# Split weights: low parts formed by a negating copy on ScalarE and an adding transfer, in place of a subtraction on VectorE

## The chip, the cores and the metric

The program runs on one core of a Trainium2 chip. The time is the device time of one execution, in microseconds; of several executions the median is given. The engines of the core work at the same time and wait for each other by semaphores: TensorE (PE for its matmuls, PEld for its weight loads), VectorE (DVE), ScalarE (ACT), GpSimd (POOL) and SyncE (SP, which only issues transfers here).

## The reference

Two request groups (512 and 256 tokens, 768 in all) go through two layers with shared weights, all in float32. Layer 0 mixes tokens with windowed attention, layer 1 with a gated convolution of width 3.

```python
for i in range(DEPTH):
    j = i // N_MIXERS
    h = rms_norm(x, norm_mix[i])
    if i % N_MIXERS == 0:
        x = x + window_attention(h, attn_w_qkv[j], attn_w_o[j], attn_sink[j], band_bias, in_window)
    else:
        x = x + short_conv(h, conv_w_in[j], conv_w[j], conv_w_out[j])
    h = rms_norm(x, norm_mlp[i])
    x = x + jnp.square(jax.nn.relu(h @ mlp_w_up[i])) @ mlp_w_down[i]
    gate = jax.nn.sigmoid(rms_norm(x, norm_ple[i]) @ ple_w_gate[i])
    x = x + (p[i] @ ple_w_proj[i]) * gate
return rms_norm(x, final_norm)
```

The model width is 1024, the hidden width of the MLP 4096, and p has 256 columns.

## The kernel before

**Split operands.** The matmuls take float32r operands. To keep float32 precision each operand is split: its high part is the value rounded to float32r, its low part is what the rounding left. A product of weight w and activation x is then three matmuls for each block of 128 rows: high w with high x, high w with low x, low w with high x, in this order (`group2`, line 123, for two halves of 384 tokens; `group`, line 131, for pieces of up to 512 tokens). The low part of a weight is so first read by the third matmul of its first block, that is the fifth matmul where the tokens are two halves.

**Weights.** A weight tile is 128 rows by up to 1024 columns. `fetch` (line 87) loads it from HBM by SP's queue into `wraw`, of which there are three. `weight` (line 92) takes two tiles, `whi` and `wlo`, of which there are two each, and calls `split` (line 81):

```python
first = act.activation(hi, src, AF.Copy)
dve.tensor_tensor(lo, src, hi.bitcast(F32), ALU.subtract)
```

ScalarE so writes the high part with a rounding copy, and VectorE the low part as raw less high. With two buffers a weight can be split while TensorE works with the one before; the split waits until TensorE has read the older tile in that buffer for the last time.

**Who calls `weight`.** With a source in HBM and the tag "w": the queries and keys of attention and the projections there, the output weights `w_o`, the last group's down-projection of each MLP (`last_down`), the gates (`ple`, and two in `last_ple`), the convolution's inputs (`mixer_conv`: products c, u and b for each of eight blocks) and its output (`project_add`). Three calls have no source, since their load was written apart at the program's start, and one has the tag "z". The other products of the MLPs form sums of weight blocks first, with splits of their own (class `Weights7`), in the same `whi` and `wlo` buffers where their tag is none; they do not call `weight`.

**What sets the order.** Each engine runs its instructions in a fixed order. In the first part of attention, in the MLPs with `last_down`, and at the end the order on ScalarE, VectorE and TensorE is that of the code; in attention, the output product, the gates and the convolution a scheduler chooses it when the program is built. In `last_down` four chunks of weights follow each other; the next chunk's split is called at the head of a chunk's turn, and in ScalarE's order it stands behind the norm (`xs_ple`, `sq`) of the two blocks of the chunk before. The norm waits for VectorE's residual add (line 813), which waits for TensorE. GpSimd sets three columns of each z to zero in the convolution (line 1330) and does nothing else behind the program's start.

Of the kernel before, what the change touches and what calls it, by code (L numbers as in the profile page):

```python
# [11 lines left out]
F32 = mybir.dt.float32  # L12
F32R = mybir.dt.float32r
AF = mybir.ActivationFunctionType
ALU = mybir.AluOpType
# [32 lines left out]
def trunk_kernel(ctx: ExitStack, tc: tile.TileContext, a: dict, out: bass.AP):  # L48
    nc = tc.nc
    act, dve, pe = nc.scalar, nc.vector, nc.tensor  # L50
# [30 lines left out]
    def split(hi, lo, src):  # L81

        first = act.activation(hi, src, AF.Copy)  # L83
        dve.tensor_tensor(lo, src, hi.bitcast(F32), ALU.subtract)  # L84
        return first.ins

    def fetch(src):
        raw = wp.tile([P, CH], F32, name="wraw", bufs=3)
        nc.sync.dma_start(raw[:, : src.shape[1]], src)
        return raw  # L90

    def weight(src, n, raw=None, tag="w"):

        m = CH if src is None else src.shape[1]
        if raw is None:
            raw = fetch(src)
        pool, bufs = (wp, 2) if tag == "w" else (more, 1)
        hi, lo = (pool.tile([P, CH], F32R, tag=f"{tag}{p}", name=f"{tag}{p}", bufs=bufs) for p in ("hi", "lo"))
        split(hi[:, :m], lo[:, :m], raw[:, :m])
        return blocks(hi[:, :m], n), blocks(lo[:, :m], n)  # L100


# [63 lines left out]
    def blocks(t, n):  # L166

        m = t.shape[1] // n
        return [t[:, i * m : (i + 1) * m] for i in range(n)]
# [284 lines left out]
    def mixer_attention():  # L454
# [52 lines left out]
        with tc.manual_schedule(engines=order):  # L507
# [24 lines left out]
            for k in range(2):  # L532
# [5 lines left out]
                part0[1].append(pl[:])  # L538
            w0 = blocks(hi[:], 2), blocks(lo[:], 2)
            w1 = weight(None, 2, raw=w1)  # L540
            for i in range(KB):
                step(0, i, (w0, w1)[i // 4], part0, "L", i % 2)
                norm.block(i, xin(i))
                if i == 3:
                    wk = weight(None, KB, raw=wk)
                    wq = [fetch(a["w_q"][0])]
# [4 lines left out]
            dve.tensor_tensor(brow[:], bp[:HEADS, :], mk[:], ALU.add)  # L551
            kps = list(products(terms_of(wk, xs)))
            wq[0] = weight(None, KB, raw=wq[0])
            ss = norm.sum_squares(psum)

# [815 lines left out]
    w = [weight(a["w_o0"][2], 4)] * 2  # L1371
# [108 lines left out]
```

## Time and profile before

| | |
|---|---|
| time, median of 3 runs | 1717.21 us (1716.59 to 1718.06) |
| span of the profiled execution | 1715.4 us |
| HBM read, written | 123.10 MB, 10.48 MB |
| PE granted clock | 0.97 to 1.00 in all stages up to 1628 us |

The stages, from the trace: start and first projection 0 to 60 us, attention 60 to 280, its output product 280 to 312, MLP of layer 0 from 312, with `last_down` from 771 to 805, gates 805 to 873, convolution 873 to 1075, its output 1075 to 1142, MLP of layer 1 1142 to 1628, gates and final norm to the end.

In the rows of the profile, a group of instructions gives line, engine, operation, the tile written and the tiles read, shapes, the count, then busy time and mean duration in ns, then idle time of the engine before them and who ended it. A row of the timeline gives start, duration, engine, line and operation, and in brackets the idle time before it with its releaser.

### The profile page before, as it was taken

How to read it: one execution, taken by the hardware profiler on the slowest of the kernel's cores; microseconds unless marked ns; L12 is line 12 of the kernel's file. 1: busy time of each engine (PE TensorE's matmuls, PEld its weight loads, DVE VectorE, ACT ScalarE, POOL GpSimd, SP SyncE). 2: the span in 40 equal slices, each digit the busy share in tenths (PEclk: the TensorE clock that was granted, in tenths of full speed). 3: DMA queues.
4: the chain of work that ended last, by engine and by line, in shares of the span. 5: the costliest groups of instructions: out<-in, count | busy, mean ns of one | idle time of the engine just before them, and what ended most of it. 6: DMA issues, size and time to landing. Idle time of an engine off the chain costs nothing.

```text
span 1715.4 us, 24192 instructions
## 1 busy us (share of the span) xinstructions
PE 1673.1 (98%) x9542; PEld 1615.8 (94%) x9542; DVE 1348.2 (79%) x2207; ACT 857.6 (50%) x1368; POOL 2.0 (0%) x30
## 2 busy tenths in 40 slices
PE   8999999989999999999999999999999999999996
PEld 7887788989999999999999999998999999999986
DVE  7587888889999999977764444658989999998776
ACT  6467756755555445445541111445455555544554
POOL 0000000000000000000000000000000000000000
PEclk9999999999999999999999999999999999999998
DMA  8653322212222122222311111211222122212222
GB/s 262 190 147 110 118 64 80 87 50 74 74 74 68 68 74 75 71 84 83 108 62 62 67 68 63 74 56 44 74 74 72 64 74 74 75 62 88 82 83 93
DMA packets 47842, 144.59 MB, mean 84 GB/s; under 512 B 6080, under 2 KB 10688, under 8 KB 47728
## 3 DMA queue, kind: packets, MB, share of 16 engines
q1 hardware_dynamic: 45168, 139.89, 24.6%
q10 hardware_dynamic: 2560, 3.15, 0.7%
q8 instruction: 75, 1.23, 0.3%
q14 instruction: 39, 0.32, 0.1%
HBM read 123.10 MB, written 10.48 MB: 78 GB/s over the span
## 4 chain that ended last, share of the span: by engine, by line
PE 66%; DVE 24%; ACT 7%; issue 2%; DMA 0%; DVEq 0%; ACTq 0%; SPq 0%
PE a L449 13%; PE mm L129 9%; PE mm L138 8%; PE gate L129 4%; PE b L129 4%; PE c L129 4%; PE u L129 4%; PE gate L138 4%; PE C L449 3%; PE B L449 3%; PE b L449 3%; DVE t L344 3%; DVE y L920 3%; DVE wlo L428 3%; DVE zlo L428 2%
## 5 line engine op out<-in xcount | busy, mean ns | idle before, releaser
L83 ACT ACTIVATE whi<-wraw 128x1024 fp32r<-128x1024 f32 (+2 forms) x73 | 75.5, 1034 | 184.8 <-PE b L129 53.0
L417 ACT ACTIVATE whi<-sum 128x1024 fp32r<-128x1024 f32 x56 | 58.9, 1052 | 146.6 <-PE a L449 146.6
L923 ACT ACTIVATE y<-y 128x768 f32<-128x768 f32 x64 | 53.7, 839 | 144.7 <-DVE y L920 144.5
L449 PE MATMUL a<-act,whi 128*128 128x384 f32 x448 | 96.7, 337 | 0.0
L449 PE MATMUL a<-t,zhi 128*128 128x384 f32 x448 | 92.3, 337 | 4.0 <-ACT c L1036 4.0
L84 DVE TENSOR_TENSOR wlo<-wraw,whi 128x1024 fp32r<-128x1024 f32 (+2 forms) x73 | 87.0, 1192 | 9.4 <-ACT whi L83 9.2
L449 PE MATMUL a<-xs,whi 128*128 128x384 f32 x448 | 88.5, 339 | 5.0 <-ACT whi L417 3.3
L449 PE MATMUL b<-t,zhi 128*128 128x384 f32 x448 | 92.4, 338 | 0.0
L449 PE MATMUL a<-t,whi 128*128 128x384 f32 x448 | 91.9, 337 | 0.0
L1092 DVE TENSOR_TENSOR x<-x,a 128x384 f32<-128x384 f32 x112 | 60.8, 553 | 33.8 <-PE a L449 33.5
L449 PEld LDWEIGHTS a<-xs,whi 128*128 128x128 f32 x448 | 79.3, 189 | 5.9 <-ACT whi L417 3.6
L449 PEld LDWEIGHTS a<-t,zhi 128*128 128x128 f32 x448 | 79.1, 188 | 4.6 <-ACT c L1036 4.6
L138 PE MATMUL mm<-xs_mix,whi 128*128 128x512 f32 (+1 forms) x320 | 82.9, 342 | 0.0
L449 PEld LDWEIGHTS b<-t,zhi 128*128 128x128 f32 x448 | 80.0, 189 | 0.0
L449 PEld LDWEIGHTS a<-act,whi 128*128 128x128 f32 x448 | 79.8, 188 | 0.0
L449 PEld LDWEIGHTS a<-t,whi 128*128 128x128 f32 x448 | 79.0, 188 | 0.0
L428 DVE TENSOR_TENSOR wlo<-sum,whi 128x1024 fp32r<-128x1024 f32 x56 | 68.4, 1222 | 9.4 <-ACT whi L417 9.4
L428 DVE TENSOR_TENSOR wlo<-wraw,whi 128x1024 fp32r<-128x1024 f32 x60 | 73.2, 1220 | 0.4 <-ACT whi L417 0.4
L417 ACT ACTIVATE whi<-wraw 128x1024 fp32r<-128x1024 f32 x60 | 63.2, 1053 | 12.0 <-PE C L449 6.5
L428 DVE TENSOR_TENSOR zlo<-sum,zhi 128x1024 fp32r<-128x1024 f32 x56 | 68.1, 1217 | 0.0
L338 ACT ACTIVATE t<-y 128x768 fp32r<-128x768 f32 x56 | 47.1, 842 | 42.0 <-DVE y L329 31.6
L417 ACT ACTIVATE zhi<-sum 128x1024 fp32r<-128x1024 f32 x56 | 59.3, 1059 | 16.5 <-DVE sum L393 16.5
(297 smaller groups left out, 4629.6 us busy)
## 6 DMA issues: line engine op xcount, KB each, us to landing
wraw<-in_up SPq DMA_DIRECT2D x64, 512.0 KB, 3.5
wraw<-in_down SPq DMA_DIRECT2D x64, 512.0 KB, 3.5
wraw<-in_w_in SPq DMA_DIRECT2D x24, 512.0 KB, 3.5
wraw<-in_gate SPq DMA_DIRECT2D x16, 512.0 KB, 3.5
pj<-pjs SPq DMA_DIRECT2D x16, 384.0 KB, 3.1
wraw<-in_w_q SPq DMA_DIRECT2D x8, 512.0 KB, 4.7
wraw<-in_w_out SPq DMA_DIRECT2D x8, 512.0 KB, 3.5
x_in<-in_x SPq DMA_DIRECT2D x8, 384.0 KB, 7.0
```

Source lines behind the costliest of these rows:

```text
L83: first = act.activation(hi, src, AF.Copy)
L84: dve.tensor_tensor(lo, src, hi.bitcast(F32), ALU.subtract)
L129: pe.matmul(t, lhsT=w, rhs=x[:, o:e], start=first and i == 0 and j == 0, stop=last and i == n - 1 and j == 2)
L138: pe.matmul(ps[:, o:e], lhsT=w, rhs=x[:, o:e], start=i == 0 and j == 0, stop=i == n - 1 and j == 2,)
L338: act.activation(t[0][:], (self.q1, self.q2)[i][:], AF.Copy)
L344: dve.tensor_tensor(lo[:], (self.q1, self.q2)[i][:], hi[:].bitcast(F32), ALU.subtract)
L417: act.activation(hi[:], src, AF.Copy)
L428: dve.tensor_tensor(lo[:], src, hi[:].bitcast(F32), ALU.subtract)
L449: pe.matmul(ps, lhsT=a, rhs=b, start=start and i == 0, stop=i == len(terms) - 1, skip_group_check=True)
L920: dve.scalar_tensor_tensor(t[:, o:e], src, 0.0, r[:, o:e], op, ALU.mult)
L923: act.activation(t[:], t[:], AF.Square)
L1092: dve.tensor_tensor(t[:, o : o + H], t[:, o : o + H], f, op)
```

## The change

In `weight`, where there is a source in HBM and the tag is "w", the low part is no longer formed by VectorE. ScalarE writes the high part as before, then writes the negated high part into the low tile; then a transfer issued by GpSimd reads the same weight from HBM again and adds it into the low tile, so that it holds raw less high. The load of `wraw` remains.

```diff
--- before.py
+++ after.py
@@ -96,7 +96,12 @@
             raw = fetch(src)
         pool, bufs = (wp, 2) if tag == "w" else (more, 1)
         hi, lo = (pool.tile([P, CH], F32R, tag=f"{tag}{p}", name=f"{tag}{p}", bufs=bufs) for p in ("hi", "lo"))
-        split(hi[:, :m], lo[:, :m], raw[:, :m])
+        if src is None or tag != "w":
+            split(hi[:, :m], lo[:, :m], raw[:, :m])
+        else:
+            act.activation(hi[:, :m], raw[:, :m], AF.Copy)
+            act.activation(lo[:, :m], hi[:, :m].bitcast(F32), AF.Copy, scale=-1.0)
+            nc.gpsimd.dma_start(lo[:, :m], src, accum_op=ALU.add)
         return blocks(hi[:, :m], n), blocks(lo[:, :m], n)
```

All later lines move down by five. 68 weights are affected: 64 of 128 by 1024, four of 128 by 768. The transfer waits for ScalarE's negated copy, for the earlier transfer on its semaphore, and the first matmul that reads the low part waits for the transfer.

ScalarE in `last_down` of layer 1, before (`act` is the last activation's split, `xs_ple` and `sq` the norm of a finished block, `whi` a chunk's high part):

```order
L83 ACTIVATE act<-y_15167 128x768
L83 ACTIVATE whi<-wraw 128x1024
L186 ACTIVATE xs_ple_15262<-x,vec 128x768
L192 ACTIVATE acc_ple_10972<-x 128x768
L186 ACTIVATE xs_ple_15281<-x,vec 128x768
L195 ACTIVATE sq<-x 128x768
L83 ACTIVATE whi<-wraw 128x1024
L186 ACTIVATE xs_ple_15324<-x,vec 128x768
```

and now:

```order
L83 ACTIVATE act<-y_15229 128x768
L102 ACTIVATE whi<-wraw 128x1024
L103 ACTIVATE wlo<-whi 128x1024
L191 ACTIVATE xs_ple_15326<-x,vec 128x768
L197 ACTIVATE acc_ple_11034<-x 128x768
L191 ACTIVATE xs_ple_15345<-x,vec 128x768
L200 ACTIVATE sq<-x 128x768
L102 ACTIVATE whi<-wraw 128x1024
L103 ACTIVATE wlo<-whi 128x1024
L191 ACTIVATE xs_ple_15389<-x,vec 128x768
```

The order is the same, with the negated copy (line 103) directly behind each high part.

ScalarE at the end of attention, before (`ot` belongs to the last attention block, `aos` are the split heads, the first `whi` is the first weight of the output product, `zhi` the weight with the tag "z", `p` a split input):

```order
L722 ACTIVATE ot<-O 64x512
L83 ACTIVATE whi<-wraw 128x1024
L83 ACTIVATE aos<-heads 128x768 x2
L83 ACTIVATE zhi<-wraw 128x1024
L83 ACTIVATE p_3378<-wraw 128x768
```

and now:

```order
L727 ACTIVATE ot<-O 64x512
L83 ACTIVATE aos<-heads 128x768 x2
L102 ACTIVATE whi<-wraw 128x1024
L83 ACTIVATE zhi<-wraw 128x1024
L103 ACTIVATE wlo<-whi 128x1024
L83 ACTIVATE p_3394<-wraw 128x768
```

Here the scheduler has moved the heads' split ahead of the weight's, and the negated copy behind `zhi`.

GpSimd from the last down-projection of layer 0 into the convolution, where before it had only the 24 instructions on z:

```order
L104 DMA wlo<-in_down 128x1024 x4
L104 DMA wlo<-in_gate 128x1024
L1335 MEMSET z 128x1 x6
L104 DMA wlo<-in_gate 128x1024 x7
L104 DMA wlo<-in_w_in 128x1024 x5
L1335 MEMSET z 128x1 x3
L104 DMA wlo<-in_w_in 128x1024 x2
```

The transfers are queued between them, in the order in which the weights are used. In attention the scheduler has also put other instructions of ScalarE, VectorE and TensorE in a somewhat different order; from the output product on TensorE's order is the one before, but for one place in the last gates.

## The prediction

> **What bounds the kernel now.** I read the totals first, then the busy times by stage, then the chain of waits, then the instructions in order of time where the changed weights are used.
>
> ```profile
> span 1715.4 us, 24192 instructions
> PE 1673.1 (98%) x9542; PEld 1615.8 (94%) x9542; DVE 1348.2 (79%) x2207; ACT 857.6 (50%) x1368; POOL 2.0 (0%) x30
> ```
>
> VectorE's 79% is an average; whether relief for it is worth anything is read by stage. In the next rows the columns are window, length, then busy time of PE, PEld, DVE, ACT and POOL, granted clock, DMA share and GB/s.
>
> ```profile
> 60.00:280.00 220.00, 210.78 (x1242) 178.24 (x1240) 181.46 (x535) 146.27 (x369) 0.00 (x0) 0.98 0.38 111
> 757.00:805.00 48.00, 48.00 (x277) 48.00 (x276) 33.46 (x45) 23.95 (x31) 0.17 (x3) 1.00 0.25 84
> 805.00:873.00 68.00, 68.00 (x391) 68.00 (x390) 49.13 (x61) 34.09 (x39) 0.16 (x3) 1.00 0.28 97
> 873.00:1075.00 202.00, 202.00 (x1158) 202.00 (x1158) 94.10 (x136) 39.86 (x42) 0.98 (x18) 1.00 0.18 63
> 1075.00:1142.00 67.00, 67.00 (x386) 67.00 (x385) 40.48 (x58) 28.47 (x36) 0.00 (x0) 1.00 0.20 71
> 1587.00:1628.00 41.00, 41.00 (x236) 41.00 (x235) 28.91 (x40) 20.84 (x26) 0.00 (x0) 1.00 0.23 76
> ```
>
> The five stages from 757 on are where 48 of the 68 changed weights are used (last down-projection, gates, convolution, its output, last down-projection again). There TensorE and its weight loads are busy for the whole window: VectorE work taken away there can gain nothing. Only in attention (60 to 280 us) is TensorE idle at all, 220 - 210.78 = 9.2 us. The chain agrees: it runs over seven gate products in one piece.
>
> ```profile
> 814.11 58.71 PE gate L129 x336
> ```
>
> So the question is what the new path of the low part costs. 336 matmuls in 58.71 us are 0.175 us each, 8.38 us for a product of 48.
>
> **What is removed and added.** Of 73 low parts on line 84, five have no source in HBM (two halves of the first projection, its second half, the first key and query weights); 68 change.
>
> ```profile
> L83 ACT ACTIVATE whi<-wraw 128x1024 fp32r<-128x1024 f32 (+2 forms) x73 | 75.5, 1034 | 184.8 <-PE b L129 53.0 <-PE u L129 51.3 <-PE c L129 27.4
> L84 DVE TENSOR_TENSOR wlo<-wraw,whi 128x1024 fp32r<-128x1024 f32 (+2 forms) x73 | 87.0, 1192 | 9.4 <-ACT whi L83 9.2
> ```
>
> VectorE loses 68 x 1.19 = 81 us; ScalarE gains 68 copies of the same shape as its high part, 68 x 1.03 = 70 us; GpSimd gains 68 issues, and the 512 KB of a weight are read from HBM a second time. Nowhere is ScalarE near its limit (50%), so its time matters by delay only. What counts is the chain: high part 1.05 us, negated copy 1.05 us behind it, then an adding transfer whose duration no row shows. I call D the time from the end of the negated copy to the first matmul that may read the low part.
>
> **The slack in the steady stages.** Two buffers hold two weights, so a weight is prepared while the product before it runs.
>
> ```profile
> 906.75 1.06 ACT L83 ACTIVATE whi<-wraw 128x1024 fp32r<-128x1024 f32 x1 [1.72 <-PE c L129]
> 915.28 0.87 PE L129 MATMUL b<-xs_mix,whi 128*128 128x384 f32 x4
> 915.98 0.51 PE L129 MATMUL b<-xs_mix,wlo 128*128 128x384 f32 x2
> ```
>
> ScalarE starts when the last user of that buffer ends. The negated copy would end at 906.75 + 2 x 1.06 = 908.87; the low part is read first at 915.98, after four matmuls on the high part. So D may be 7.1 us at no cost, in some 40 products. Beyond that an excess is paid in every second product only: a product that waits also lengthens the time in which the next weight is prepared. The cost is 40 x (D - 7.1)/2.
>
> **The price of the transfer**, from the nearest rows:
>
> ```profile
> q1 hardware_dynamic: 45168, 139.89, 24.6%
> wraw<-in_w_in SPq DMA_DIRECT2D x24, 512.0 KB, 3.5
> pj<-pjs SPq DMA_DIRECT2D x16, 384.0 KB, 3.1
> wraw<-in_w_v SPq DMA_DIRECT2D x2, 384.0 KB, 8.1
> skew<-brow SPq DMA_DIRECT2D x1, 1022.0 KB, 12.0
> ```
>
> Below: a plain load of the same bytes, 3.5 us. Queue q1 spent 0.246 x 16 x 1715.4 = 6752 engine-us on 139.89 MB, so 0.524 MB over 16 engines take 1.6 us of the 3.5 and 1.9 us are fixed. An addition must read the destination too: 1.9 + 2 x 1.6 = 5.1. A load and a store one after the other would be 3.5 + 3.1 = 6.6. I take the middle, D = 5.8; the upper ends are 8.1 (a load among many) and 12.0 (the longest transfer here). GpSimd issues no transfer in this trace, so its own share is inside these bounds.
>
> The Trainium skill, "DMA: Bandwidth & Descriptors", section "Anatomy of one DMA", gives a transfer issued from GpSimd about 2.0 us and bytes over 436 GB/s, which for 512 KB would be an estimated 3.2 us; no run here shows such a transfer yet, and the plain load's 3.5 is near it. "Collectives: The Full Stack", section "The bandwidth ceiling", says that an add in the DMA path needs two source reads on one ring, which would make it an estimated 4.4 us. By the first the change would be hidden nearly everywhere; by the second its sum would be under half of mine.
>
> **Where the slack is shorter.** In the last down-projection ScalarE's order is fixed by hand, and a chunk's high part stands behind the norm of the chunk before:
>
> ```profile
> 764.61 1.06 ACT L83 ACTIVATE whi<-wraw 128x1024 fp32r<-128x1024 f32 x1 [0.97 <-PE c L449]
> 772.04 0.51 PE L129 MATMUL mm<-act,wlo 128*128 128x384 f32 x2
> 774.35 1.04 ACT L83 ACTIVATE whi<-wraw 128x1024 fp32r<-128x1024 f32 x1
> 780.43 0.51 PE L129 MATMUL mm<-act,wlo 128*128 128x384 f32 x2
> 783.24 1.04 ACT L83 ACTIVATE whi<-wraw 128x1024 fp32r<-128x1024 f32 x1
> 784.43 1.22 DVE L84 TENSOR_TENSOR wlo<-wraw,whi 128x1024 fp32r<-128x1024 f32 x1
> 788.80 0.51 PE L129 MATMUL mm<-act,wlo 128*128 128x384 f32 x2
> 792.02 1.05 ACT L83 ACTIVATE whi<-wraw 128x1024 fp32r<-128x1024 f32 x1
> 797.17 0.51 PE L129 MATMUL mm<-act,wlo 128*128 128x384 f32 x2
> ```
>
> Slack is the low part's first use less two copies: 772.04 - 766.7 = 5.3; 780.43 - 776.4 = 4.0; 788.80 - 785.3 = 3.5; 797.17 - 794.1 = 3.1, and for the last one 1.1 more, because the subtraction at 784.43, which stood ahead of the residual adds that ScalarE waits for, is gone: 4.2. A wait at one chunk gives the next that much more room, so at D = 5.8 the waits are 5.8 - 5.3 = 0.5; 5.8 - 4.0 - 0.5 = 1.3; 5.8 - 3.5 - 1.3 = 1.0; 5.8 - 4.2 - 1.0 = 0.6: together 3.4 us, and 6.8 for the two layers, whose order is the same. Behind TensorE nothing else can fill these waits: its next matmul needs the low part, and all later products queue behind it.
>
> The second layer's gates run on 512 tokens first:
>
> ```profile
> 1620.49 1.04 ACT L83 ACTIVATE whi<-wraw 128x1024 fp32r<-128x1024 f32 x1
> 1628.81 0.39 PE L138 MATMUL gate<-xs_ple,wlo 128*128 128x512 f32 x1
> 1628.25 1.06 ACT L83 ACTIVATE whi<-wraw 128x1024 fp32r<-128x1024 f32 x1
> 1634.38 0.40 PE L138 MATMUL gate<-xs_ple,wlo 128*128 128x512 f32 x1
> ```
>
> The first has 6.2 us (no wait), the second 1634.38 - 1630.4 = 4.0: 1.8 us.
>
> The end of attention:
>
> ```profile
> 273.47 1.04 ACT L83 ACTIVATE whi<-wraw 128x1024 fp32r<-128x1024 f32 x1
> 274.48 1.58 ACT L83 ACTIVATE aos<-heads 128x768 fp32r<-128x768 f32 x2
> 273.60 0.85 DVE L727 TENSOR_TENSOR heads<-O,ot 64x256 f32<-64x256 f32 x2
> 274.55 1.23 DVE L84 TENSOR_TENSOR wlo<-wraw,whi 128x1024 fp32r<-128x1024 f32 x1
> 280.59 0.94 PE L129 MATMUL mm<-aos,whi 128*128 128x384 f32 x4 [1.19 <-DVE xa L743]
> 281.37 0.51 PE L129 MATMUL mm<-aos,wlo 128*128 128x384 f32 x2
> ```
>
> The new order has aos, the high part, zhi and then the negated copy: 274.45 + 1.5 + 3 x 1.05 = 279.1. The product could start some 0.6 us earlier, near 280.0, and read the low part at 280.8: slack 1.7, wait 5.8 - 1.7 = 4.1 us. The other attention weights are split several microseconds ahead of use; I put them at nothing, and without that cover each would cost its missing part.
>
> **Relief in attention.** 18 subtractions go; the one at 274.55 stands on the chain (1.2 us). Bounds: all of TensorE's idle time, -9.2, and on the other side two of the 18 copies that ScalarE gains landing on the chain, 2 x 1.05, +2. I take -1.2, the row that is on the chain. GpSimd's own work, the zeroing of z, is 0.98 us in the convolution's window; in its queue it now stands between the transfers, waits for VectorE's reading of an older z, and I put it at nothing; if that were late, the next transfer would be late with it.
>
> **Sum** at D = 5.8: 6.8 + 1.8 + 4.1 - 1.2 = 11.5 us. The profiled execution's span is 1715.4, the median of the runs 1717.2; I add to the latter: 1728.7 us.
>
> **The rivals.**
> 1. The transfer outlasts the steady slack. For it: nothing bounds an adding transfer from above here, and GpSimd writes the requests. Against: 7.1 us is twice a plain load. At D = 8.1: chunks 2 x 8.0, gates 1.0 + 3.1, attention 6.4, steady 40 x 1.0/2 = 20, less 1.2: +45, 1762. At D = 12.0: +147, 1864.
> 2. The transfer is hidden (D of 3.5 to 4.3). At 3.5 only the end of attention waits, 1.8 - 1.2 = +0.6; at 4.3 +3.3: 1718 to 1720. For it: a plain load lands in 3.5 us. Against it: the second read and the issue by GpSimd both add to that. The Trainium skill's figure for a transfer from GpSimd, above, belongs here.
> 3. Faster: attention is held by VectorE's queue (181.46 of 220 us), and 18 subtractions fewer let TensorE close its idle time. It decides if the gain there exceeds the waits above, so only with D near 3.5 to 5: at best 1717.2 - 9.2 + 1.8 = 1710. Against it: VectorE has few long pieces on the chain, and one subtraction among them.
>
> That the change does nothing of what it says is excluded: the order shows 68 transfers on GpSimd and the subtractions gone.
>
> **How the numbers follow.** No change means within 0.2% (3.4 us), about what a measurement of this kernel can tell. Forecast, D from 4.3 to 7.1 (1720.5 to 1736.5): 0.50. Rival 1: 0.27. Rival 2: 0.13. Rival 3: 0.10. Slower is the forecast and rival 1, 0.77; same 0.13; faster 0.10. The range goes from halfway into rival 3, 1714, to D = 9, some 1785, and leaves out about 0.15; the forecast's own range is 1720 to 1737.
>
> **What would show it.** TensorE's first low matmul of a product in the last down-projection, of the second gate of layer 1 and of the first output product after attention waits for a DMA, some 0.5 to 4 us each, a dozen waits in all; from 873 to 1142 TensorE stays without a gap; the adding transfers land in 5 to 6 us; VectorE's busy time falls by 81 us and ScalarE's rises by 70. The prediction is wrong if the transfers take over 7 us (waits in every second convolution product), under 4.3, or if attention moves by more than 3 us.

## The result, and the profile after

The changed kernel takes 1766.1 us (1764.6 to 1767.8, four runs) against 1717.0 before: a ratio of 1.0286, with a 95% interval of 1.0271 to 1.0300. It is slower, as forecast, but by 49 us where 11.5 were forecast. Here and below, the medians and ratios leave out one execution, of the run with one gate alone, which took 3326 us.

The totals of the changed kernel:

```profile
span 1762.8 us, 24366 instructions
PE 1684.5 (96%) x9542; PEld 1622.9 (92%) x9542; DVE 1278.0 (72%) x2139; ACT 926.1 (53%) x1436; POOL 61.8 (4%) x98
```

VectorE's busy time fell by 70 us (81 forecast) and ScalarE's rose by 68.5; the time did not fall. GpSimd's 60 us are 68 issues of 0.88 us. The new transfers, with size and median time from issue to landing:

```profile
wlo<-in_w_in POOLq DMA_DIRECT2D x24, 512.0 KB, 5.8
wlo<-in_gate POOLq DMA_DIRECT2D x10, 512.0 KB, 6.2
wlo<-in_down POOLq DMA_DIRECT2D x8, 512.0 KB, 5.9
wlo<-in_w_q POOLq DMA_DIRECT2D x7, 512.0 KB, 8.1
DMA to landing us min/median/max: 4.6/6.0/9.6
```

Busy times by stage, the stages moved to where they now lie (columns as in the prediction: window, length, PE, PEld, DVE, ACT, POOL, clock, DMA share, GB/s):

```profile
60.00:280.00 220.00, 200.52 (x1211) 173.42 (x1211) 156.98 (x499) 149.18 (x364) 11.43 (x13) 0.97 0.53 136
784.00:831.00 47.00, 43.67 (x238) 42.73 (x237) 23.42 (x34) 25.50 (x29) 4.41 (x5) 0.96 0.51 126
831.00:903.00 72.00, 70.02 (x392) 69.70 (x391) 40.14 (x51) 41.55 (x46) 7.35 (x14) 0.98 0.62 154
903.00:1106.00 203.00, 202.80 (x1159) 201.72 (x1158) 67.59 (x110) 64.93 (x66) 22.05 (x42) 1.00 0.54 125
1106.00:1176.00 70.00, 67.84 (x385) 66.85 (x384) 33.31 (x50) 35.81 (x43) 6.14 (x7) 1.00 0.51 121
1621.00:1668.00 47.00, 43.03 (x242) 41.74 (x241) 25.75 (x36) 27.86 (x34) 4.38 (x5) 1.00 0.53 127
```

Attention holds 10 us less of TensorE's work in the same window (210.78 before); the last down-projections now stand idle 3 to 4 us each; the convolution (903 to 1106) is still full. The waits of TensorE that are new or much longer (total, times, longest):

```profile
PE S L679 <- DMA q<-ql: 9.4, 2, 8.7
PE mm L134 <- DMA wlo<-in_down: 7.3, 7, 2.0
PE gate L143 <- DMA wlo<-in_gate: 5.8, 1, 5.8
PE mm L143 <- DMA wlo<-in_w_q: 5.3, 2, 4.1
PE S L679 <- DVE mx L681: 4.3, 2, 3.5
PE mm L134 <- DMA wlo<-in_w_o: 2.7, 1, 2.7
PE mm L134 <- DMA wlo<-in_w_out: 2.1, 2, 1.1
PE gate L134 <- DMA wlo<-in_gate: 2.0, 1, 2.0
```

Most of the largest waits are for low parts. The largest is not: scores (`S`) that wait for queries on their way through HBM. How much later the same TensorE instructions start than before shows where the 47.4 us of span come from; each figure is the growth of that delay over the stage:

| stage | predicted | grew by |
|---|---|---|
| attention, to the output product's first matmul | -1.2 | 16.5 |
| output product after attention | 4.1 | 4.6 |
| last down-projections, both | 6.8 | 10.8 |
| gates of layer 0, convolution, its output | 0 | 3.8, 1.1, 3.0 |
| first two gates of layer 1 | 1.8 | 8.1 |

### The profile page after: what moved, and what is told of

It is laid out like the page before. It is cut to its first block, busy times and chain, and to the rows that moved or that the text cites. A ratio compares the mean times of both kernels' runs of the same rounds, so it can differ in the third digit from the quotient of the medians.

```text
span 1762.8 us, 24366 instructions
## 1 busy us (share of the span) xinstructions
PE 1684.5 (96%) x9542; PEld 1622.9 (92%) x9542; DVE 1278.0 (72%) x2139; ACT 926.1 (53%) x1436; POOL 61.8 (4%) x98
## 4 chain that ended last, share of the span: by engine, by line
issue 66%; PE 23%; DMA 5%; ACT 3%; DVE 2%; POOL 1%; DVEq 0%; SPq 0%; ACTq 0%; POOLq 0%
PE mm L143 5%; PE mm L134 3%; PE c L134 3%; PE u L134 3%; PE gate L134 2%; PE gate L143 2%; PE b L134 2%; DMA wlo<-in_gate 1%; POOL wlo L104 1%; DMA wlo<-in_w_q 1%; DMA q<-ql 1%; PE pt L714 1%; PE O L724 0%; ACT L L701 0%; DMA wlo<-in_w_in 0%
## 5 line engine op out<-in xcount | busy, mean ns | idle before, releaser
L102 ACT ACTIVATE whi<-wraw 128x1024 fp32r<-128x1024 f32 (+1 forms) x68 | 71.1, 1046 | 177.6 <-PE u L134 48.3
L103 ACT ACTIVATE wlo<-whi 128x1024 fp32r<-128x1024 f32 (+1 forms) x68 | 71.1, 1046 | 2.2 <-issue 0.4
L422 ACT ACTIVATE whi<-wraw 128x1024 fp32r<-128x1024 f32 x60 | 63.2, 1053 | 11.5 <-PE C L454 6.5
L343 ACT ACTIVATE t<-y 128x768 fp32r<-128x768 f32 x56 | 47.1, 842 | 41.9 <-DVE y L334 31.6
L422 ACT ACTIVATE zhi<-sum 128x1024 fp32r<-128x1024 f32 x56 | 59.3, 1060 | 16.5 <-DVE sum L398 16.5
```

The costliest lines, as they stand in the source:

```text
L102: act.activation(hi[:, :m], raw[:, :m], AF.Copy)
L103: act.activation(lo[:, :m], hi[:, :m].bitcast(F32), AF.Copy, scale=-1.0)
L343: act.activation(t[0][:], (self.q1, self.q2)[i][:], AF.Copy)
L422: act.activation(hi[:], src, AF.Copy)
```

## The experiments

In most of them `weight` gets a switch `add`, on by default in some runs and off in others, and a few calls set it; only that edit is shown. Growths of TensorE's delay are counted as in the table above.

**The change outside attention only.** The 18 weights of attention and right behind it keep the subtraction:

```diff
-                w = wq[0] if c == 0 else weight(a["w_q"][c], KB, raw=wq[1] if c == 1 else None)
+                w = wq[0] if c == 0 else weight(a["w_q"][c], KB, raw=wq[1] if c == 1 else None, add=False)
...
```

> The change only for the 50 weights of the last down-projections, the gates, the convolution and its output; the 18 weights of attention and of what follows it at once keep the subtraction. By my prediction's terms (6.8 for the last down-projections, 1.8 for the second gate of layer 1, nothing elsewhere): 1717.0 + 8.6 = 1726. By the difference of the two traces (5.7 and 5.1 in the last down-projections, 3.8 and 8.1 in the gates, 1.1 and 3.0 in convolution and output): 1717.0 + 27 = 1744. If the parts hang together, attention's lateness being what slows the rest, it would be well under 1744.

Measured: 1743.5 us, ratio 1.0155 (1.0140 to 1.0170). The 25.9 us are the trace's 27, three times my 8.6.

**The change in attention only.** The same calls, the other way round:

```diff
-                w = wq[0] if c == 0 else weight(a["w_q"][c], KB, raw=wq[1] if c == 1 else None)
+                w = wq[0] if c == 0 else weight(a["w_q"][c], KB, raw=wq[1] if c == 1 else None, add=True)
...
```

> The change only for the 18 weights of attention and of the products right after it. By my prediction's terms (4.1 - 1.2): 1717.0 + 2.9 = 1720. By the difference of the two traces (about 16.5 up to the end of attention and 4 in the first output product): 1717.0 + 21 = 1738. If the parts add up, this one and the run of the other 50 together have the change's 49 us.

Measured: 1738.7 us, ratio 1.0122 (1.0104 to 1.0139): 21.2 us. 25.9 + 21.2 = 47.1 of 49: the losses are local and add up, so attention could be studied by itself.

**ScalarE's copy without the transfer.**

```diff
-            nc.gpsimd.dma_start(lo[:, :m], src, accum_op=ALU.add)
+            dve.tensor_tensor(lo[:, :m], raw[:, :m], lo[:, :m].bitcast(F32), ALU.add)
```

> All 68 weights with ScalarE's negated copy, but the raw weight is added to it by VectorE, with no transfer: ScalarE's 70 us and the longer chain stay, VectorE's relief, the second read and the transfer's time are gone. If the transfer is the cause of the loss (its time or its traffic): within 6 us of before, 1717 to 1723. If ScalarE's additional copies, or another order of the instructions in attention that comes with them, are the cause there: 1732 or more, with attention longer by over 10 us.

Measured: 1724.8 us, ratio 1.0046 (1.0031 to 1.0061): 7.2 us (1724.78 against 1717.56), between the two expectations. The second copy and the longer chain cost something (TensorE's work in 60 to 280 us falls by 4.5 us, second row of the next view), a seventh of the loss. Nearly all of it arises in attention: TensorE's delay grows by 7.4 us there, where the change has 16.5. So a good part of attention's loss comes without any transfer; the part on the prediction shows where.

**Everything but the wait, in attention.** The products read VectorE's low part; beside it the new low part is formed and not used:

```diff
         split(hi[:, :m], lo[:, :m], raw[:, :m])
+        if add and src is not None and tag == "w":
+            shadow = shadows.tile([P, CH], F32R, tag="shadow", name="shadow", bufs=2)
+            act.activation(shadow[:, :m], hi[:, :m].bitcast(F32), AF.Copy, scale=-1.0)
+            nc.gpsimd.dma_start(shadow[:, :m], src, accum_op=ALU.add)
```

> The kernel before, with the 15 weights used within attention also formed in the new way in two tiles of their own that nothing reads (ScalarE's negated copy, GpSimd's adding transfer from HBM); the products read VectorE's low part. The traffic, ScalarE's copies and GpSimd's issues are there, the wait for the transfer is not. If the lateness of the low parts makes the loss in attention (17 us): 1717 to 1722. If the second read slows the other transfers (q, k, bias, raw weights) or the copies hold ScalarE: 1730 or more.

Measured: 1719.8 us, ratio 1.0016 (1.0006 to 1.0026): 2.3 us. In this program the second read, the copies and the issues are nearly free, since nobody waits for them. It doesn't show that the low parts' lateness is all of attention's loss: the scheduler's order of TensorE's instructions there is another one than in the change. The windows 60 to 280 us of the run with the change in attention, of ScalarE's copy without the transfer, and of this one:

```profile
60.00:280.00 220.00, 201.13 (x1208) 174.03 (x1207) 156.43 (x497) 148.42 (x361) 11.43 (x13) 0.96 0.55 137
60.00:280.00 220.00, 206.24 (x1205) 174.57 (x1204) 176.34 (x528) 155.34 (x377) 0.00 (x0) 0.98 0.38 109
60.00:280.00 220.00, 207.73 (x1220) 175.15 (x1219) 176.97 (x529) 155.01 (x379) 12.39 (x14) 0.98 0.56 140
```

The first and the third have nearly the same DMA share and GpSimd time; TensorE's work differs by 6.6 us (the third is the trace of the slowest of ten executions, 1724.7 us).

**One early weight back on VectorE.**

```diff
+ ... weight(a["w_q"][c], KB, raw=wq[1] if c == 1 else None, add=c != 1)
```

> The change for all but one weight: the second query weight, the first of all to be changed, keeps VectorE's subtraction. In the changed kernel its product stood 4.1 us at 50 us for the transfer and went on at half the clock, and what follows began 7.3 us later than before. If such delays simply add up along TensorE's order: 1766.1 - 7 = 1759. If attention has slack that takes this delay up, or the later weights wait by as much more: 1764 to 1766.

Measured: 1758.1 us, ratio 1.0249 (1.0228 to 1.0270): 8.0 us less than with it (four executions, from 1753.5 to 1764.2). One weight of 68 holds about a sixth of the loss.

**A plain load in place of the adding one.**

```diff
-            nc.gpsimd.dma_start(lo[:, :m], src, accum_op=ALU.add)
+            nc.gpsimd.dma_start(lo[:, :m], src.bitcast(F32R))
```

> The changed kernel with a plain load in place of the adding one, from the same queue of GpSimd behind the same negated copy: the low part is the raw weight, the sum is left out. If the addition's second read makes the transfer long (1.6 us in my prediction's price), the transfers land in about 4.4 us instead of 6.0, the waits in the last down-projections and the gates go and the time falls to about 1740. If issue and queue make it long: landings of 5.5 to 6 us and 1760 to 1766.

Measured: 1747.3 us, ratio 1.0182 (1.0161 to 1.0203). This kernel leaves the sum out: its low part is the raw weight. Its landings:

```profile
wlo<-in_w_in POOLq DMA_DIRECT2D x24, 512.0 KB, 4.6
wlo<-in_w_q POOLq DMA_DIRECT2D x7, 512.0 KB, 8.2
```

In the steady stage the addition costs 5.8 - 4.6 = 1.2 us. In attention it costs nothing that the median shows (8.1 against 8.2): there the transfer is long because of the others beside it. TensorE's work in 60 to 280 us stays at 199.8, so the 19 us gained lie outside attention, and attention's loss does not depend on the addition.

**A third pair of buffers in attention,** with the change (15 weights) and without it:

```diff
+        if third is not None and src is not None:
+            turns += 1
+            if turns % 3 == 0:
+                pool, bufs = third, 1
```

> The change in attention alone (15 weights), with a third pair of buffers there for high and low parts, so that a weight may be prepared one product earlier. To be read against the same buffers without the change (next run). If the low parts are late because their buffer comes free late: within 5 us of that run. If ScalarE's place for the copies in its order, or the transfers' length, sets it: 12 us or more above that run.

> The kernel before with the third pair of buffers in attention and VectorE's subtraction everywhere: the control for the run before this one. Both theories: 1712 to 1722.

Measured: 1723.8 us with the change, ratio 1.0034 (1.0022 to 1.0046); 1713.6 without, ratio 0.9978 (0.9968 to 0.9987). The change costs 10.2 us over its control, between the two expectations, and some 16.6 with two pairs (21.2 less the output product's 4.6). The scores' longest wait for queries is gone in the run with the change:

```profile
PE S L689 <- DMA q<-ql: 2.1, 2, 1.3
```

The third pair moves the scheduler's order too, so buffers and order are not told apart by these two runs. The control is the fastest kernel of this study, 0.2% below the one before.

**The same, with the second query weight back on VectorE:**

```diff
-                ... weight(a["w_q"][c], KB, raw=wq[1] if c == 1 else None, add=True)
+                ... weight(a["w_q"][c], KB, raw=wq[1] if c == 1 else None, add=c != 1)
```

> Attention alone, with the third pair of buffers, and the second query weight back on VectorE: 14 weights changed. That weight had the only long wait left in the run with the third pair (3.7 us at about 50 us, and the slower clock behind it). If the loss in attention is that one wait and the buffers that come free late: 1713.6 + 0 to 3, so 1714 to 1717. If there is a further cost of the change in attention (ScalarE's copies, the traffic): 1720 or more.

Measured: 1717.3 us, ratio 1.0003 (0.9994 to 1.0013): 6.6 us less than with that weight, 3.7 above the control. So attention's loss is that one wait (6.6 to 8.0 us), what the program with a third pair takes away (some 6, by its buffers or by its order), and a rest of 3.7, near the 2.3 that the unread low parts cost.

**One gate alone:**

```diff
-                w = weight(a["gate"][1, m], KB)
+                w = weight(a["gate"][1, m], KB, add=m == 1)
```

> The change for one weight alone, the second gate of layer 1, whose transfer took 9.6 us in the changed kernel, beside four loads of raw gate weights. By my prediction (transfer and start 5.8 us, slack 4.0): 1717.3 + 1.8 = 1719. By the trace (wait 5.8 us, and 2.3 us more until the clock is back): 1717.3 + 8 = 1725.

Measured: 1722.4 us, ratio 1.0028 (1.0017 to 1.0039): 5.3 us, between the two. Its transfer took 7.2 us instead of 9.6 and TensorE waited 3.1. My formula with that duration gives 7.2 + 0.3 - 4.0 = 3.5: the formula holds, the one value for the transfer does not. The traced execution took 1720.5 us, 3.3 more than before; why the median of seven is 2 us above that, no trace shows.

**The convolution alone:**

```diff
-            group2(cp, terms_of(weight(a["w_in"][KB + m], KB), norm.xs))
+            group2(cp, terms_of(weight(a["w_in"][KB + m], KB, add=True), norm.xs))
...
```

> The change for the convolution's 24 weights alone. By my prediction's slack of 7.1 us: no change, 1716 to 1719. If transfers in the steady stages cost by their length in every second product: at 8.1 us of delay 24 x 1.0/2 = 12 more, 1729.

Measured: 1718.6 us, ratio 1.0008 (0.9998 to 1.0017): no change that can be measured. The slack of 7.1 us hides these 24 transfers.

**The negated copy first.**

```diff
-            act.activation(hi[:, :m], raw[:, :m], AF.Copy)
-            act.activation(lo[:, :m], hi[:, :m].bitcast(F32), AF.Copy, scale=-1.0)
+            act.activation(lo[:, :m], raw[:, :m], AF.Copy, scale=-1.0)
             nc.gpsimd.dma_start(lo[:, :m], src, accum_op=ALU.add)
+            act.activation(hi[:, :m], raw[:, :m], AF.Copy)
```

> All 68 weights changed, but ScalarE forms the negated copy first, from the raw weight, and the high part behind it, so that each transfer starts 1.05 us earlier with the same work. If lateness makes the loss: 1.05 us less at each of the dozen places outside attention that wait, some 7 to 10 us in all, 1756 to 1760. If the work itself costs (ScalarE, traffic): 1766.

Measured: 1794.6 us, ratio 1.0449 (1.0433 to 1.0465): 28 us slower than the change, against both expectations. Landings in this run, then the raw load and the adding transfer of one weight each, first of the change, then of this run:

```profile
wlo<-in_w_in POOLq DMA_DIRECT2D x24, 512.0 KB, 7.6
wraw<-in_w_in SPq DMA_DIRECT2D x24, 512.0 KB, 4.1
```

```profile
946.88 0.33 SPq L89 DMA_DIRECT2D wraw<-in_w_in  x1
948.35 0.87 POOL L104 DMA_DIRECT2D wlo<-in_w_in  x1 [7.49 <-ACT wlo L103]
```

```profile
948.06 0.33 SPq L89 DMA_DIRECT2D wraw<-in_w_in  x1
948.44 0.89 POOL L103 DMA_DIRECT2D wlo<-in_w_in  x1 [6.48 <-ACT wlo L102]
```

In the convolution the scheduler put the high part ahead of the negated copy all the same (its buffer comes free earlier), so no transfer started earlier. But the negated copy now reads `wraw` too, and frees it only at its end: the next raw load starts 0.4 us before the adding transfer instead of 1.5 us. The raw load then runs beside the adding transfer for its whole length. The adding transfer grows from 5.8 to 7.6 us, past the slack, the raw load from 3.5 to 4.1, and the convolution's products wait (162.47 us of TensorE's work in 906 to 1073 us, where the change has 166.80). That is my first rival's mechanism. By TensorE's delay 9 of the 28 us arise in the convolution and 10 in its output. That the 1.1 us of difference between the two issues started it is read from these rows; it wasn't varied alone.

## Why the prediction was right or wrong

**What bounds the kernel, and the steady slack: right.** TensorE bounds it from 757 us on, VectorE's relief was worth nothing, and the convolution alone costs nothing. With 5.8 us from issue and 0.4 us from the copy's end to the issue, D is 6.2 there, under 7.1.

But the 7.1 us hold only where the negated copy stands directly behind the high part; I took that for all 40 products. In the convolution's output the scheduler put three or four instructions of a norm between the two copies of the second, fourth and sixth weight:

```profile
1114.35 1.06 ACT L102 ACTIVATE whi<-wraw 128x1024 fp32r<-128x1024 f32 x1 [5.25 <-PE mm L134]
1117.89 1.04 ACT L103 ACTIVATE wlo<-whi 128x1024 fp32r<-128x1024 f32 x1
1124.88 0.61 PE L134 MATMUL mm<-ys,wlo 128*128 128x384 f32 x2 [1.13 <-DMA wlo<-in_w_out]
```

The transfer took only 5.5 us; the slack was 4.8 us instead of 7.1, and TensorE waited 1.1. A wait in every second product is what the formula has, but this is another cause. At one gate of layer 0 an instruction between the copies and a transfer of 7.9 us came together, and TensorE waited 2.0. Gates, convolution and output grew by 7.9 us where I had nothing.

**The step that failed: "The other attention weights are split several microseconds ahead of use; I put them at nothing."** With the end of attention's relief of 1.2 this made -1.2, and 16.5 were measured: over 17 of the 38 us missing, and one of my signs of being wrong. No row stood behind it. The second query weight shows it:

```profile
42.00 1.02 POOL L104 DMA_DIRECT2D wlo<-in_w_q  x1 [40.70 <-ACT wlo L103]
50.14 1.01 PE L143 MATMUL mm<-xs_mix,wlo 128*128 128x512 f32 x2 [4.09 <-DMA wlo<-in_w_q]
```

It landed 8.1 us after its issue; before, VectorE had that low part ready at 41 us. With the slower clock behind the wait, TensorE's delay grows by 7 us here; with this weight alone back on VectorE the time fell by 8.0 and 6.6.

Another 7 us need no transfer. I bounded the cost of ScalarE's copies in attention by 2 us, and gave the scheduler's new order nothing. In the change, and in the run with ScalarE's copies and no transfer, VectorE waits at one place for `bias`, whose load ScalarE issues, and the scores (`S`) wait for VectorE; the kernel before has no wait there. The change, then the run without the transfer:

```profile
133.20 0.48 DVE L681 CUSTOM_DVE_ANT_0 L<-S,bias,sink 128x256 f32<-128x256 f32 x1 [2.87 <-DMA bias<-skew]
133.75 0.69 PE L679 MATMUL S<-khh,q 128*128 128x384 f32 x1 [3.54 <-DVE mx L681]
```

```profile
124.65 0.48 DVE L681 CUSTOM_DVE_ANT_0 L<-S,bias,sink 128x256 f32<-128x256 f32 x1 [3.03 <-DMA bias<-skew]
125.19 0.69 PE L679 MATMUL S<-khh,q 128*128 128x384 f32 x1 [2.10 <-DVE mx L681]
```

In both the clock is 0.50 in the next 4 us. In the run without the transfer TensorE's delay grows by 8 us around this place and is 7.4 at the end of attention. So of the 16.5 us some 7 come with the first wait, some 7 also come without any transfer, and some 2 are left. That the parts add up in this way was not tried, nor whether the copies or the order of the instructions make the second. In the run with the third pair and the change VectorE waits 2.8 us for `bias` as well, but TensorE has products to run meanwhile.

Later in attention a wait can stand behind one more stage: queries go through HBM, and while the seventh query weight's adding transfer ran (172.1 to 181.2 us), so did these (number of issues, size, median landing, in 165 to 182 us):

```profile
xa<-in_x SPq DMA_DIRECT2D x2, 384.0 KB, 8.5
wlo<-in_w_q POOLq DMA_DIRECT2D x1, 512.0 KB, 9.1
q<-qh SPq DMA_DIRECT2D x2, 192.0 KB, 8.6
q<-ql SPq DMA_DIRECT2D x2, 192.0 KB, 8.3
```

The queries' 3.2 us of before became 8.3, and the scores waited 8.7. That this transfer alone made it wasn't tried; with the unread low parts the queries' loads kept a median of 3.0 and 3.4. Though it is the longest wait, little of it is left at the end of attention: counted by position, since the orders differ, TensorE's delay was 17 us ahead of it and is 16.5 there.

**One value for D: mis-sized.** 5.8 us was near the quiet stages (6.2 with the issue), but a transfer beside a burst takes 8 to 10. The last gates have such a burst, visible in the program before, since four raw gate weights are loaded there one behind the other:

```profile
1668.94 6.52 SPq L89 DMA_DIRECT2D wraw<-in_gate  x4
1670.42 0.89 POOL L104 DMA_DIRECT2D wlo<-in_gate  x1 [8.14 <-ACT wlo L103]
1680.03 0.80 PE L143 MATMUL gate<-xs_ple,wlo 128*128 128x512 f32 x1 [5.83 <-DMA wlo<-in_gate]
```

9.6 us of transfer, so a wait of 5.8 instead of 1.8.

The Trainium skill, "DMA: Bandwidth & Descriptors", section "Issuing engines are not separate DMA queues", says that transfers of all engines run on the same 16 DMA engines and interleave; these rows agree. The Trainium skill's section "Anatomy of one DMA" on the same page, cited in the prediction, gave an estimated 3.2 us for these bytes from GpSimd; the plain load measured 4.6 and the adding one 5.8, so the measurement decides.

**A wait costs more than its length.** The waits in the last down-projections were sized rightly in sum, 7.3 us where I had 6.8, though not one by one (2.0 us at one chunk, where I had at most 1.3). The delay grew by 10.8, in part because TensorE's clock is lower behind some of them. Windows behind the last gate's wait (the clock is the third figure from the end):

```profile
1676.00:1680.00 4.00, 0.00 (x0) 0.00 (x0) 2.01 (x3) 3.53 (x5) 0.00 (x0) 0.68 0.91 249
1680.00:1684.00 4.00, 3.97 (x9) 3.15 (x10) 1.88 (x4) 1.15 (x2) 0.00 (x0) 0.50 0.01 3
1684.00:1688.00 4.00, 4.00 (x19) 3.39 (x18) 0.29 (x1) 0.00 (x0) 0.00 (x0) 0.97 0.00 0
```

9 matmuls in four microseconds, then 19: the 5.8 us of wait cost 8.1. No term of the prediction had this. The clock was also lower behind a wait of 2.0 us in the down-projection (0.58 over the next 4 us), but not behind several of 0.3 to 1.0, and not behind the 3.1 us in the traced execution with one gate. The Trainium skill, "TensorE: Matmul & The Clock Gate", section "What's actually happening", has a clock halved after an idle window of about 3.4 us that runs freely, and full again after as much work; the half clock for 4 us agrees. The wait of 2.0 us does not: it is shorter than such a window and lowered the clock all the same, so there the measurement decides. What separates it from the wait of 3.1 us is not shown.

**The output product after attention: the number right, by luck,** 4.1 predicted, 4.6 grown.

```profile
301.08 0.61 PE L134 MATMUL mm<-aos,wlo 128*128 128x384 f32 x2 [2.74 <-DMA wlo<-in_w_o]
```

D was 7.1 us, not 5.8 (copy's end 293.99, landing 301.04). The slack was 4.4, not 1.7: TensorE's order is not the one of before here, against the text on the change, since two matmuls on `zhi` stand ahead of the low part's. The wait was 2.7, and the clock of 0.61 in the 4 us behind it makes up most of the rest.

**The rivals.** The first one's number (1762) is near the result, its mechanism isn't the cause: its largest term was the steady stages. The second (hidden) is excluded by landings of 5.8 us and waits in every tight place. The third (faster) is excluded: TensorE's idle time in attention doubled (9.2 to 19.5 us). So none of them is the cause. The forecast's mechanism, waits where slack is short, is, except for some 7 us of attention's loss, which come without a transfer too. Its number fell with the step on attention, the clock, and the sizes above.

## What to carry to other kernels

A transfer in place of an engine's instruction is priced by where its reader stands: 24 in a stage with 7.1 us of slack were free, and one beside a burst cost 5 to 8 us. Make the table of slack for every use, the first stage and the scheduled ones above all, and read beside each which other transfers start within its time. Where a scheduler sets the order, read what it puts between the instructions that you take for neighbours, and run the engine's additional work without the transfer: here that alone cost 7 us. To a wait of several microseconds on TensorE add the slower clock behind it.

## What the runs showed of the hardware

In three places an adding transfer was held back until the one before had landed, and it is the program that does this. ScalarE finished two negated copies 2 us apart (at 130.92 and 132.95); in the changed kernel the second issue came only when the first had landed (131.32 + 8.2 = 139.52):

```profile
131.32 0.87 POOL L104 DMA_DIRECT2D wlo<-in_w_q  x1 [32.97 <-ACT wlo L103]
139.88 0.89 POOL L104 DMA_DIRECT2D wlo<-in_w_q  x1 [7.68 <-DMA wlo<-in_w_q]
```

The records of GpSimd's semaphores in this trace show the reason: at 139.86 us GpSimd passes a wait for semaphore 115, the one that the transfer issued at 131.32 counts up, and issues the second right behind it. So the earlier transfer that the text on the change speaks of is here the one just before. With plain loads from the same queue both were issued at once, and GpSimd's wait for semaphore 115 stands behind the second issue (136.98):

```profile
128.72 0.53 POOL L104 DMA_DIRECT2D wlo<-in_w_q  x1 [33.08 <-ACT wlo L103]
130.75 0.53 POOL L104 DMA_DIRECT2D wlo<-in_w_q  x1 [1.50 <-ACT wlo L103]
```

The same happened at 301 us and at 861 us, where the issue came 2.8 and 1.1 us after its copy's end instead of 0.4, and in the runs with the change in attention alone and with the unread low parts. Why the program places the wait so was not tried. An adding transfer's issue takes GpSimd 0.88 us, a plain one's 0.53.
